# A decoder step on one core: the first x tile's v columns in plain fp32, and a new order of the start

## The chip, the cores and the metric

The kernel runs on one core of a Trainium2 chip. The metric is device time in microseconds (us); of several runs the median counts.

## The reference

`reference()` computes one layer of a hybrid decoder for a prompt of 1024 tokens and for 8 single sample tokens with saved state. All of it is float32, the model width is 1024.

```python
hn = rmsnorm(x, g_norm)                 # x * rsqrt(mean(x*x) + 1e-6) * g_norm
u = hn @ w_in                           # 1024 x 7176: xa za q k v o zb, then 8 gate columns
yA, ... = rglru_branch(xa, ...)         # convolution, two gates, linear recurrence
hB, ... = mlstm_seq(q, k, v, ig, lf, ...)   # 4 heads, chunks of 128 tokens
merged = concat([yA * silu(za), rms(sigmoid(o) * hB) * g_mhead * silu(zb)])
y = rmsnorm(x + merged @ w_out, g_final)
```

The change touches the norm and the first 256 + 256 columns of v (`v0`, `v1`) together with the 8 gate columns.

## The kernel before

**Numbers.** Most products are made of three passes: each float32 operand is split into a rounded high part (a cast on ACT, line 70) and a low part (a subtraction on DVE, line 71), and TensorE adds high·high, high·low and low·high (`mm3`, lines 64 to 66, or `plain`, line 531). A float32 operand that is not split goes through TensorE as it is; the trace then shows two records for each matmul that isn't a transpose.

**The first unit.** The input projection runs in units of two column blocks of 256. Units 1 to 13 use a scheme with seven products on quadrants of x and w (`product`); the seven splits of x quadrants and of their sums stand in `cb`. Unit 0 (`v0 v1`) is computed tile by tile while x is still being normalised: `plain(i, w)` multiplies token tile i (128 tokens) with column block w, and its block w = 0 carries the 8 gate columns as well (264 columns). It is 24 matmuls, k chunks 0 to 3 and then 4 to 7.

**Preparing a tile.** The eight tiles come in the order 4 0 5 1 6 2 7 3 (`xorder`; n counts places in it). `x_fetch(n)` loads a tile. `x_stats(n)` squares it on ACT, takes the root, and finishes the reciprocal root on DVE (n = 0, 1) or on POOL (`rsqrt_early`, n > 1). `x_scale(n)` multiplies by that and by the broadcast g_norm on DVE. `x_turn(n)` transposes it on TensorE in two halves of four. `x_splits(n)` splits the transposed halves from PSUM. `x_copy` copies the halves of a tile i >= 4 for later sums; `x_combos(i)` makes the sums that `product` needs (one subtraction for i >= 4, three for i < 4), and `x_out` splits these. For the first tile the scaling is in `x_turn(0)` (line 425), straight from the PSUM tiles `gn_p` in which a matmul with a row of ones spreads g_norm over all partitions (line 560); `gn_b` is the copy of them for the later tiles.

**What sets the order.** From line 561 to line 638 PE, DVE and ACT run in the order in which the code issues the instructions (`manual_schedule`). In step m of the loop at line 581 `plain(i, 0)` comes first, then the next tile's transposes and splits, then `plain(i, 1)`, and between them statistics, sums and their splits. Before line 561 and after line 638, and on SP and POOL throughout, a list scheduler places the instructions as they become ready. Loads go over SP's DMA queue (`ld`), stores over POOL's (`stq`); only the two halves of g_norm's row go over ACT's queue (line 373). The x tiles and the split weights of block 1 (`w1`) share a ring of six buffers (`ws`).

**The sample tokens.** In steps 2 to 4 the 8 sample tokens are normalised too (`sample_turn`, `sample_square`, `sample_sum`, `sample_scale`, `sample_out`); the last one writes `hnd` on DVE (line 461), which the matmuls of line 604 in step 4 read.

Of the kernel before, what the change touches and what calls it, by code (L numbers as in the profile page):

```python
# [9 lines left out]
F32 = mybir.dt.float32  # L10
# [7 lines left out]
P = 128  # L18
T = 1024
HT = 512  # L20
# [29 lines left out]
def hymba_kernel(  # L50
# [17 lines left out]
    def split(hi, lo, src):  # L68

        A.copy(hi, src)  # L70
        V.tensor_tensor(lo, src, hi.bitcast(F32), op=ALU.subtract)  # L71
# [9 lines left out]
    def ps(tag, shape):  # L81
        return psp.tile(shape, F32, tag=tag, name=f"ps_{tag}", bufs=NBUF.get(tag, 1))
# [13 lines left out]
    def ws(shape, name, dt=F32R):  # L96

        return wsp.tile(shape, dt, tag="ws", name=name)
# [8 lines left out]
    def dconst(shape, name):  # L107

        return dpool.tile(shape, F32, tag=name, name=name)
# [98 lines left out]
    def load_raw(u, b, parts=(0, 1)):  # L208

        if u >= len(units):  # L210
            return
        if (u, b) not in raws:
            raws[u, b] = rawp.tile([P, 4, 512], F32, tag=f"raw{b}", name=f"raw{b}_{u}")
        for a in parts:
            kind, j = units[u][a]
            c = COL[kind] + j * 256
            ld(raws[u, b][:, :, a * 256:(a + 1) * 256],
               w_in[0, b * HT:(b + 1) * HT, c:c + 256].rearrange("(k p) c -> p k c", p=P))
# [151 lines left out]

    gn_r = [sg([1, HT], f"gn_r{n}") for n in range(2)]
    for n in range(2):
        nc.scalar.dma_start(gn_r[n], g_norm[:, n * HT:(n + 1) * HT])
    warm = const([P, 1], "warm")
    A.activation(warm, ones[:, 0:1], AF.Sqrt)
    es_f = ExitStack()
# [4 lines left out]
    xorder = [4, 0, 5, 1, 6, 2, 7, 3]  # L381
    xt, xps, bf = {}, {}, {}

    def x_fetch(n):

        i = xorder[n]
        xt[i] = fp.tile([P, T], F32, tag="x2", name=f"x{i}") if n % 3 == 2 else ws([P, T], f"x{i}", F32)
        ld(xt[i], x_prompt[0, i * P:(i + 1) * P, :])

    def x_scale(n):  # L390
        x = xt[xorder[n]]
        V.scalar_tensor_tensor(x, x, st0[:, 1, n:n + 1], gn_b, op0=ALU.mult, op1=ALU.mult)
# [11 lines left out]
    def x_stats(n):  # L404

        ss, r, t = (st0[:, j, n:n + 1] for j in range(3))
        junk = sg([P, T], "junk", BF16)
        A.activation(junk, xt[xorder[n]], AF.Square, accum_out=ss)
        if n > 1:
            rsqrt_early(r, ss, t)  # L410
            return
        A.activation(r, ss, AF.Sqrt, scale=1.0 / T, bias=eps_t)
        V.tensor_scalar(ss, ss, 1.0 / T, EPS, op0=ALU.mult, op1=ALU.add)
        V.reciprocal(r, r)
        V.tensor_tensor(t, r, r, op=ALU.mult)
        V.scalar_tensor_tensor(t, t, -0.5, ss, op0=ALU.mult, op1=ALU.mult)
        V.scalar_tensor_tensor(r, t, 1.5, r, op0=ALU.add, op1=ALU.mult)
# [45 lines left out]
    def x_split(i, half):  # L463

        p = xps[i][half]
        s = slice(i % 4 * P, (i % 4 + 1) * P)
        if i >= 4 and half == 0:
            bf[i] = [fp.tile([P, 4, P], F32R, tag=f"b12{n}", name=f"b12{n}") for n in "hl"]
            split(*bf[i], p)
        else:  # L470
            q = Q_P3 if i >= 4 else (Q_P1, Q_P2)[half]
            split(cb[q][0][:, :, s], cb[q][1][:, :, s], p)

    def x_copy(i):

        bf["f"] = [sg([P, 4, P], f"b{n}2f") for n in (1, 2)]
        for f, p in zip(bf["f"], xps[i]):
            A.copy(f, p)

    def x_combos(i):  # L480

        p0, p1 = xps[i]
        f0, f1 = bf["f"]
        if i >= 4:
            t3 = sg([P, 4, P], "t3")
            V.tensor_tensor(t3, f1, f0, op=ALU.subtract)
            return [(Q_P7, t3)]
        t1, t2, t4 = (sg([P, 4, P], f"t{n}") for n in (1, 2, 4))
        V.tensor_tensor(t1, f0, p0, op=ALU.subtract)
        V.tensor_tensor(t2, f1, t1, op=ALU.subtract)  # L490
        V.tensor_tensor(t4, p1, t2, op=ALU.subtract)
        return [(Q_P6, t2), (Q_P5, t1), (Q_P4, t4)]

    def x_out(i, ts):

        s = slice(i % 4 * P, (i % 4 + 1) * P)
        for q, t in ts:
            split(cb[q][0][:, :, s], cb[q][1][:, :, s], t)
# [3 lines left out]
    wg = fp.tile([P, KC, 8], F32, tag="wg", name="wg")  # L502
    w1 = []

    def w1_split(b):

        t = ws([P, 4, 256], f"w1h{b}"), ws([P, 4, 256], f"w1l{b}")
        split(t[0], t[1], raws[0, b][:, :, 256:512])
        w1.append(t)

    gs = dconst([P, NCH, 8], "gs")

    def plain(i, w):

        s = slice(i % 4 * P, (i % 4 + 1) * P)
        op = []
        for k in range(KC):
            if i < 4:
                op.append([t[:, k % 4, s] for t in cb[Q_P1 if k < 4 else Q_P2]])
            elif k < 4:  # L520
                op.append([t[:, k, :] for t in bf[i]])
            else:
                op.append([t[:, k % 4, s] for t in cb[Q_P3]])
        pt = ps("o", [P, 512])[:, 0:264 - 8 * w]
        todo = [(k0, x, y) for k0 in (0, 4) for x, y in ((0, 0), (1, 0), (0, 1))]
        if w == 0 and i == xorder[0]:
            todo[1], todo[2] = todo[2], todo[1]
        for k0, x, y in todo:
            for k in range(k0, k0 + 4):
                wt = (hi, lo)[y][:, k, :] if w == 0 else w1[k // 4][y][:, k % 4, :]  # L530
                TE.matmul(pt, op[k][x], wt, start=(k, x, y) == (0, 0, 0), stop=(k, x, y) == (7, 0, 1), skip_group_check=True)  # L531

        def evac():
            t = fp.tile([P, 256], F32, tag="pe", name="pe", bufs=2)
            A.copy(t, pt[:, 0:256])
            if w == 0:
                V.tensor_tensor(gs[:, i, :], pt[:, 256:264], bgate, op=ALU.add)
            stq(d_v[w][i * P:(i + 1) * P, :], t)
        return evac

    pw = ps("tr", [P, P])

    x_fetch(0)
    load_raw(0, 0, (0,))
    ld(wg, w_in[0, :, C_G:C_G + 8].rearrange("(k p) c -> p k c", p=P))
    load_raw(0, 1, (0,))
    load_raw(0, 0, (1,))
    x_fetch(1)
    load_raw(0, 1, (1,))
    ld(xs8, x_sample.rearrange("b o (k p) -> (b o k) p", p=P))  # L550
    ld(g8, g_norm.rearrange("o (k p) -> (o k) p", p=P))
    x_fetch(2)
    ld(bgate[:, 0:4], b_mi[0].partition_broadcast(P))
    ld(bgate[:, 4:8], b_mf[0].partition_broadcast(P))
    x_fetch(3)
    for n in range(10):
        TE.matmul(pw, ones, ones, start=True, stop=True)
        if n == 6:
            for half in range(2):
                TE.matmul(gn_p[half], ones[0:1, :], gn_r[half], start=True, stop=True)  # L560
    ms_ = tc.manual_schedule(engines={mybir.EngineType.PE, mybir.EngineType.DVE, mybir.EngineType.Activation})
# [2 lines left out]
    def w0_split(k):  # L564
        split(hi[:, k:k + 2, 0:256], lo[:, k:k + 2, 0:256], raws[0, k // 4][:, k % 4:k % 4 + 2, 0:256])

    def x_splits(n):
        for half in range(2):
            x_split(xorder[n], half)
    x_stats(0)  # L570
    for half in range(2):
        A.copy(gn_b[:, half * HT:(half + 1) * HT], gn_p[half])
    x_turn(0)
    w0_split(0)
    split(hi[:, :, 256:264], lo[:, :, 256:264], wg)
    w0_split(2)
    x_splits(0)
    w0_split(4)
    w0_split(6)
    ts = []  # L580
    for m, i in enumerate(xorder):
        pe0 = plain(i, 0)
        if m == 0:
            x_stats(1)
            x_scale(1)
            w1_split(0)
            w1_split(1)
        else:
            if m + 2 < 8:
                x_stats(m + 2)  # L590
            if i >= 4:
                x_copy(i)
            else:
                ts = x_combos(i)
        if m + 1 < 8:
            x_turn(m + 1)
        if m == 2:
            sample_turn()
        if m == 3:
            sample_sum()  # L600
        if m == 4:
            pgd = ps("o", [P, 512])[0:32, 0:8]
            for k in range(KC):
                TE.matmul(pgd, hnd[:, k, 8:40], wg[:, k, :], start=k == 0, stop=k == KC - 1)
            dec_unit(0)
            load_raw(1, 0)
            load_raw(1, 1)
        if m + 1 < 8:
            x_splits(m + 1)
        pe0()  # L610
        if m == 2:
            sample_square()
        if m == 3:
            sample_scale()
        if m == 4:
            gd = dconst([NB, 8], "gd")
            V.tensor_tensor(gd, pgd[0:NB], bgate[0:NB], op=ALU.add)
            ld(d_gd, gd)
        if m == 7:
            prep(1, Q_P1)  # L620
        pe1 = plain(i, 1)
        if m == 0:
            x_stats(2)
            x_copy(i)
        if 1 < m + 2 < 8:
            x_scale(m + 2)
        if i >= 4:
            ts = x_combos(i)
        x_out(i, ts)
        pe1()  # L630
        if m == 3:
            sample_out()
        if m < 4:
            x_fetch(m + 4)
# [1026 lines left out]
```

## Time and profile before

| | |
|---|---|
| median of 3 runs | 933.48 us (932.17 to 935.03) |
| profiled execution, device time | 934.05 us |
| its span | 932.3 us |
| PE busy | 919.0 us, 99% of the span |
| PE weight loads (beside PE) | 760.4 us, 82% |
| DVE busy | 706.6 us, 76% |
| ACT busy | 575.4 us, 62% |
| POOL busy | 155.7 us, 17% |
| chain that ended last | PE 92%, DVE 2%, ACT 2%, DMA 2%, issue 1% |

The span goes from the first to the last instruction of the profiled execution; 1.75 us of its device time lie outside. The chain is followed back from the last instruction to what released each one. Times in the rows count from the start of the span.

### The profile page before, as it was taken

To read this page: it belongs to the slowest core of one execution; us is meant where nothing else is said; L and a number is where in the kernel's file an instruction comes from. 1 tells how busy PE (TensorE), PEld (TensorE's weight loads), DVE (VectorE), ACT (ScalarE), POOL (GpSimd) and SP (SyncE) were. 2 spreads that over 40 slices of the span, in tenths; PEclk is the share of its full clock that TensorE was granted. 3 is DMA by queue.
4 is the path that set the end of the run, shared out by engine and by line. 5 is a ranking of instruction groups with operands and counts; after the bars stand their busy time and mean duration, and the time that the engine had idled before them with its cause. 6 is when DMAs were issued, how large, how long until landed. Compare 5 with 4: busy or idle time off the path is not lost.

```text
span 932.3 us, 15295 instructions
## 1 busy us (share of the span) xinstructions
PE 919.0 (99%) x5313; PEld 760.4 (82%) x5313; DVE 706.6 (76%) x1460; ACT 575.4 (62%) x1034; POOL 155.7 (17%) x290
## 2 busy tenths in 40 slices
PE   9999999999999999999999999999999999999996
PEld 7997687878787988687789898876687888888886
DVE  5765887899888888989788866688757677667754
ACT  6743456767686668588577773447636466556642
POOL 1420111011211222222112212010201000000110
PEclk9999999999999999999999999999999999999999
DMA  6341364344566466457726562534963664465431
GB/s 216 107 130 63 128 202 159 119 158 152 186 195 202 164 227 224 154 170 262 229 79 222 175 202 92 170 141 171 346 184 119 161 187 147 126 182 164 122 84 48
DMA packets 131191, 153.17 MB, mean 164 GB/s; under 512 B 15660, under 2 KB 110004, under 8 KB 131106
## 3 DMA queue, kind: packets, MB, share of 16 engines
q1 hardware_dynamic: 113382, 96.32, 34.6%
q0 software_dynamic: 17728, 55.87, 16.5%
q8 instruction: 42, 0.69, 0.3%
q14 instruction: 35, 0.29, 0.1%
q10 hardware_dynamic: 4, 0.00, 0.0%
HBM read 100.58 MB, written 51.65 MB: 163 GB/s over the span
## 4 chain that ended last, share of the span: by engine, by line
PE 92%; DVE 2%; ACT 2%; DMA 2%; issue 1%; SPq 0%; POOL 0%; DVEq 0%; ACTq 0%
PE ps_o L64 14%; PE ps_o L66 14%; PE ps_o L65 14%; PE ps_kv L64 11%; PE ps_kv L66 10%; PE ps_kv L65 10%; PE ps_o L531 4%; PE ps_tr L234 3%; PE ps_s L866 2%; PE ps_s L1196 2%; PE ps_qp L1028 1%; PE ps_tr L1333 1%; PE ps_qp L64 1%; PE ps_qp L65 1%; PE ps_qp L66 1%
## 5 line engine op out<-in xcount | busy, mean ns | idle before, releaser
L70 ACT CAST wh<-raw 128x1024 fp32r<-128x1024 f32 x91 | 95.3, 1048 | 74.8 <-PE ps_o L65 21.0
L71 DVE TENSOR_TENSOR wl<-raw,wh 128x1024 fp32r<-128x1024 f32 x91 | 111.0, 1221 | 35.7 <-ACT wh L70 20.1
L64 PE MATMUL ps_kv<-cb_hi,wh 128*128 128x512 f32 x320 | 126.8, 396 | 0.0
L66 PE MATMUL ps_kv<-cb_hi,wl 128*128 128x512 f32 x320 | 125.3, 391 | 0.0
L65 PE MATMUL ps_kv<-cb_lo,wh 128*128 128x512 f32 x320 | 125.2, 391 | 0.0
L64 PE MATMUL ps_o<-cb_hi,wh 128*128 128x512 f32 x240 | 94.6, 394 | 0.0
L66 PE MATMUL ps_o<-cb_hi,wl 128*128 128x512 f32 x240 | 93.6, 390 | 0.0
L65 PE MATMUL ps_o<-cb_lo,wh 128*128 128x512 f32 x240 | 93.6, 390 | 0.0
L64 PEld LDWEIGHTS ps_kv<-cb_hi,wh 128*128 128x128 f32 x320 | 60.1, 188 | 17.8 <-issue 3.4
L66 PEld LDWEIGHTS ps_kv<-cb_hi,wl 128*128 128x128 f32 x320 | 60.1, 188 | 13.3 <-issue 0.4
L65 PEld LDWEIGHTS ps_kv<-cb_lo,wh 128*128 128x128 f32 x320 | 60.2, 188 | 12.4 <-issue 0.4
L64 PE MATMUL ps_kv<-wh,cb_hi 128*128 128x256 f32 x192 | 54.9, 286 | 0.5 <-ACT s L325 0.5
L66 PE MATMUL ps_kv<-wh,cb_lo 128*128 128x256 f32 x192 | 54.6, 284 | 0.0
L65 PE MATMUL ps_kv<-wl,cb_hi 128*128 128x256 f32 x192 | 54.5, 284 | 0.0
L64 PEld LDWEIGHTS ps_o<-cb_hi,wh 128*128 128x128 f32 x240 | 45.1, 188 | 11.5 <-issue 2.1
L64 PE MATMUL ps_o<-wo,mh 128*128 128x512 f32 (+1 forms) x136 | 53.2, 392 | 1.0 <-ACT mh L70 1.0
L66 PEld LDWEIGHTS ps_o<-cb_hi,wl 128*128 128x128 f32 x240 | 45.1, 188 | 9.7
L64 PE MATMUL ps_o<-wo,rh 128*128 128x512 f32 (+1 forms) x136 | 52.9, 389 | 0.0
L65 PEld LDWEIGHTS ps_o<-cb_lo,wh 128*128 128x128 f32 x240 | 45.1, 188 | 9.1
L66 PE MATMUL ps_o<-wo,rl 128*128 128x512 f32 (+1 forms) x136 | 51.8, 381 | 0.0
L65 PE MATMUL ps_o<-wo,rh 128*128 128x512 f32 (+1 forms) x136 | 51.7, 380 | 0.0
L65 PE MATMUL ps_o<-wo,mh 128*128 128x512 f32 (+1 forms) x136 | 51.5, 380 | 0.0
(492 smaller groups left out, 2447.0 us busy)
## 6 DMA issues: line engine op xcount, KB each, us to landing
raw<-in_w_in_dram SPq DMA_DIRECT2D x56, 512.0 KB
Cb<-in_state_mlstm_C_dram SPq DMA_DIRECT2D x32, 256.0 KB
out_dram<-Cb POOLq DMA_DIRECT2D x32, 256.0 KB, 4.5
qk<-d_qk SPq DMA_DIRECT2D x32, 256.0 KB
oraw<-in_w_out_dram SPq DMA_DIRECT2D x16, 512.0 KB
d_qk<-s POOLq DMA_DIRECT2D x24, 256.0 KB, 3.0
x<-in_x_prompt_dram SPq DMA_DIRECT2D x8, 512.0 KB
d_x<-s POOLq DMA_DIRECT2D x16, 256.0 KB, 3.0
```

The lines of the kernel that those rows point to most:

```text
L64: TE.matmul(out, ah, bh, start=first, stop=False, skip_group_check=True)
L65: TE.matmul(out, ah, bl, start=False, stop=False, skip_group_check=True)
L66: TE.matmul(out, al, bh, start=False, stop=last, skip_group_check=True)
L70: A.copy(hi, src)
L71: V.tensor_tensor(lo, src, hi.bitcast(F32), op=ALU.subtract)
L234: TE.matmul(dz_["p"][32 * g:32 * g + 32, :], hnd[:, k, 0:32] if second else hnd[:, k, 8:40], raws[u, k // 4][:, k % 4, :], start=k < 4 and ...
L531: TE.matmul(pt, op[k][x], wt, start=(k, x, y) == (0, 0, 0), stop=(k, x, y) == (7, 0, 1), skip_group_check=True)
L866: TE.matmul(pg, w[:, n, :], st["xx"][n], start=k == 0, stop=k == 1)
L1028: TE.matmul(pq[32 * g:32 * g + n, 0:256], qsel[:, kb, 4 * bb:4 * bb + n], ds_["C", h * NB + bb][:, kb, :], start=bb < 2, stop=bb >= NB - 2 ...
L1196: TE.matmul(S, qk[:, 2 + kb, :], qk[:, kb, :], start=kb == 0, stop=kb == 1)
L1333: TE.matmul(dec_o[0][32 * g:32 * g + 32, :], md, oraw[m][:, half * 512:(half + 1) * 512], start=first and m in ms[:2], stop=last and m in ...
```

## The change

Nothing changes in the kernel after the start (the loop over units and all that follows). In the start:

- The first tile (tile 4, place 0) goes through both blocks of unit 0 in one function, `first_tile`: its two transposed halves, copied from PSUM as float32, are the stationary operands, and the loaded weights `raws[0, b]` and `wg` the moving ones, none of them split. It is 16 float32 matmuls of 256 columns and 8 of the 8 gate columns, in place of `plain(4, 0)` and `plain(4, 1)`. The weights are still split for the other seven tiles, but `split` of block 1 is taken apart into `w1_hi` and `w1_lo`. Of the first tile only the second half is split (it goes into `cb[Q_P3]`, from the copy).
- g_norm's row is loaded over SP's queue, first in it; the first x tile goes over ACT's queue. The second x tile stands ahead of the weights of block 1. Seven warm-up matmuls in place of ten, and the broadcast of g_norm after five in place of seven.
- The transposes of the second tile come behind `first_tile`.
- In the loop (now steps 1 to 7), `x_combos(i)` and `x_stats(m + 2)` stand later: the statistics behind the next tile's splits, the sums behind `plain(i, 1)`. The first tile's sum is made early and split in step 1.

```diff
     for n in range(2):
-        nc.scalar.dma_start(gn_r[n], g_norm[:, n * HT:(n + 1) * HT])
+        ld(gn_r[n], g_norm[:, n * HT:(n + 1) * HT])
...
-    x_fetch(0)
+    x_fetch(0, nc.scalar.dma_start)
     load_raw(0, 0, (0,))
     ld(wg, w_in[0, :, C_G:C_G + 8].rearrange("(k p) c -> p k c", p=P))
     load_raw(0, 1, (0,))
+    x_fetch(1)
     load_raw(0, 0, (1,))
-    x_fetch(1)
     load_raw(0, 1, (1,))
+    x_fetch(2)
...
-    for n in range(10):
+    for n in range(7):
         TE.matmul(pw, ones, ones, start=True, stop=True)
-        if n == 6:
+        if n == 4:
             for half in range(2):
                 TE.matmul(gn_p[half], ones[0:1, :], gn_r[half], start=True, stop=True)
...
+    def w1_hi(b):
+        t = ws([P, 4, 256], f"w1h{b}"), ws([P, 4, 256], f"w1l{b}")
+        A.copy(t[0], raws[0, b][:, :, 256:512])
+        w1.append(t)
+
+    def w1_lo(b):
+        h, l = w1[b]
+        V.tensor_tensor(l, raws[0, b][:, :, 256:512], h.bitcast(F32), op=ALU.subtract)
...
+    def first_tile():
+        f = bf["f"]
+        pt = [ps("o", [P, 512])[:, 0:264 - 8 * (1 - w)] for w in range(2)]
+        for w in range(2):
+            for k in range(KC):
+                TE.matmul(pt[w][:, 0:256], f[k // 4][:, k % 4, :], raws[0, k // 4][:, k % 4, w * 256:(w + 1) * 256],
+                          start=k == 0, stop=k == KC - 1 and w == 0, skip_group_check=True)
+        for k in range(KC):
+            TE.matmul(pt[1][:, 256:264], f[k // 4][:, k % 4, :], wg[:, k, :], start=False, stop=k == KC - 1, skip_group_check=True)
+        return pt
...
     x_turn(0)
     w0_split(0)
+    x_copy(i0)
+    ts0 = x_combos(i0)
     split(hi[:, :, 256:264], lo[:, :, 256:264], wg)
     w0_split(2)
-    x_splits(0)
+    x_stats(1)
+    x_scale(1)
     w0_split(4)
     w0_split(6)
+    split(cb[Q_P3][0][:, :, 0:P], cb[Q_P3][1][:, :, 0:P], bf["f"][1])
+    pt0 = first_tile()
+    x_turn(1)
+    w1_hi(0)
+    x_stats(2)
+    x_splits(1)
+    w1_hi(1)
+    x_scale(2)
+    w1_lo(0)
+    w1_lo(1)
+    evac0(i0, 0, pt0[0], None)
+    evac0(i0, 1, pt0[1], pt0[1])
+    x_fetch(4)
     for m, i in enumerate(xorder):
+        if m == 0:
+            continue
         pe0 = plain(i, 0)
-        if m == 0:
-            x_stats(1)
-            x_scale(1)
-            w1_split(0)
-            w1_split(1)
-        else:
-            if m + 2 < 8:
-                x_stats(m + 2)
-            if i >= 4:
-                x_copy(i)
-            else:
-                ts = x_combos(i)
+        if i >= 4:
+            x_copy(i)
         if m + 1 < 8:
             x_turn(m + 1)
...
         if m + 1 < 8:
             x_splits(m + 1)
         pe0()
+        if m + 2 < 8:
+            x_stats(m + 2)
...
         pe1 = plain(i, 1)
-        if m == 0:
-            x_stats(2)
-            x_copy(i)
-        if 1 < m + 2 < 8:
+        ts = x_combos(i)
+        if m + 2 < 8:
             x_scale(m + 2)
-        if i >= 4:
-            ts = x_combos(i)
         x_out(i, ts)
+        if m == 1:
+            x_out(i0, ts0)
         pe1()
```

## Rows read from the trace of the kernel before

**Rows 1.** The page: busy time of each engine (share, instructions); granted clock in slices.
```profile
PE 919.0 (99%) x5313; PEld 760.4 (82%) x5313; DVE 706.6 (76%) x1460; ACT 575.4 (62%) x1034; POOL 155.7 (17%) x290
...
PEclk9999999999999999999999999999999999999999
```

**Rows 2.** Timeline, first 24 us, PE: start, us, engine, line, out<-in, shape, count.
```profile
1.14 3.36 PE L557 MATMUL ps_tr<-ones 128*128 128x128 f32 x14 [1.14 <-POOL ones L115]
...
4.43 3.78 PE L560 MATMUL ps_o<-gn_r,ones 1*128 1x512 f32 x4
...
9.58 1.91 PE L429 MATMUL ps_kv<-idF,x 128*128 128x128 f32 x8
...
11.31 1.25 PE L531 MATMUL ps_o<-wph,b12h 128*128 128x264 f32 x4
...
13.24 1.07 PE L531 MATMUL ps_o<-wph,b12l 128*128 128x264 f32 x4
...
14.12 0.67 PE L531 MATMUL ps_o<-wph,cb_hi 128*128 128x264 f32 x4
...
14.63 0.65 PE L531 MATMUL ps_o<-wph,cb_lo 128*128 128x264 f32 x4
...
16.74 0.66 PE L429 MATMUL ps_s<-idF,x 128*128 128x128 f32 x4 [0.98 <-DVE x L392]
...
20.54 0.65 PE L531 MATMUL ps_o<-wph,cb_hi 128*128 128x264 f32 x4
...
23.44 1.04 PE L429 MATMUL ps_kv<-idF,x 128*128 128x128 f32 x8
```

**Rows 3.** Timeline, first 10 us: SP's queue, ACT and DVE.
```profile
0.75 0.40 SPq L388 DMA_DIRECT2D x<-in_x_prompt_dram  x1
...
1.52 1.28 ACT L375 ACT_TABLE_LOAD   x1 [1.52 <-PEq L1647]
...
4.35 1.06 ACT L408 ACTIVATE junk<-x 128x1024 bf16<-128x1024 f32 x1 [1.33 <-DMA x<-in_x_prompt_dram]
...
6.57 0.16 DVE L417 SCALAR_TENSOR_TENSOR st<-st 128x1 f32<-128x1 f32 x1
...
8.24 0.59 ACT L572 COPY gn_b<-ps_o 128x512 f32<-128x512 f32 x1 [1.12 <-PE ps_o L560]
...
8.86 0.75 DVE L425 SCALAR_TENSOR_TENSOR x<-x,st,ps_o 128x512 f32<-128x512 f32 x1 [0.96 <-ACT gn_b L572]
```

**Rows 4.** Timeline at 169 and 568 us, PE: unsplit float32 matmuls and what follows.
```profile
169.47 0.51 PE L918 MATMUL ps_s<-dxs,graw 128*128 128x8 f32 x4
...
169.83 0.49 PE L64 MATMUL ps_o<-cb_hi,wh 128*128 128x512 f32 x1
...
567.86 0.60 PE L1196 MATMUL ps_s<-qk 128*128 128x128 f32 x4
...
568.30 0.38 PE L1198 MATMUL ps_s<-idF,qk 128*128 128x128 f32 x2
```

**Rows 5.** Timeline at 28 us, PE: step 2's `plain`.
```profile
28.64 0.76 PE L531 MATMUL ps_o<-wph,b12l 128*128 128x264 f32 x4 [0.80 <-DVE b12l L71]
```

**Rows 6.** Timeline, 38 to 47 us: step 3 and the start of step 4.
```profile
38.38 1.04 PE L429 MATMUL ps_kv<-idF,x 128*128 128x128 f32 x8
...
39.02 0.59 ACT L70 CAST b12h<-ps_kv 128x512 fp32r<-128x512 f32 x1 [1.13 <-PE ps_kv L429]
...
39.43 0.69 DVE L491 TENSOR_TENSOR t<-ps_qp,t 128x512 f32<-128x512 f32 x1
...
42.10 1.28 DVE L392 SCALAR_TENSOR_TENSOR x<-x,st,gn_b 128x1024 f32<-128x1024 f32 x1
...
43.29 1.89 DVE L71 TENSOR_TENSOR cb_lo<-t,cb_hi 128x512 fp32r<-128x512 f32 x3
...
45.28 0.27 DVE L461 TENSOR_TENSOR hnd<-dqC,dW 128x64 f32<-128x64 f32 x1
...
46.23 0.64 PE L604 MATMUL ps_o<-wg,hnd 128*32 128x8 f32 x15
```

More of the change, by code (lines that the diff above doesn't have):

```diff
@@ L382, in hymba_kernel, with x_fetch @@
     xt, xps, bf = {}, {}, {}
-    def x_fetch(n):
+    def x_fetch(n, ld=ld):
         i = xorder[n]
@@ L503, in hymba_kernel, with evac0 @@
     w1 = []
[L505 to L509, printed above, removed]
     gs = dconst([P, NCH, 8], "gs")
+    def evac0(i, w, pt, pg):
+        t = fp.tile([P, 256], F32, tag="pe", name="pe", bufs=2)
+        A.copy(t, pt[:, 0:256])
+        if pg is not None:
+            V.tensor_tensor(gs[:, i, :], pg[:, 256:264], bgate, op=ALU.add)
+        stq(d_v[w][i * P:(i + 1) * P, :], t)
     def plain(i, w):
@@ L524, in plain @@
         pt = ps("o", [P, 512])[:, 0:264 - 8 * w]
[L525 to L528, printed above, removed]
+        for k0, x, y in [(k0, x, y) for k0 in (0, 4) for x, y in ((0, 0), (1, 0), (0, 1))]:
             for k in range(k0, k0 + 4):
@@ L531, in plain @@
                 TE.matmul(pt, op[k][x], wt, start=(k, x, y) == (0, 0, 0), stop=(k, x, y) == (7, 0, 1), skip_group_check=True)
[L533 to L539, printed above, removed]
+        return lambda: evac0(i, w, pt, pt if w == 0 else None)
     pw = ps("tr", [P, P])
-    x_fetch(0)
+    x_fetch(0, nc.scalar.dma_start)
     load_raw(0, 0, (0,))
@@ L546, in hymba_kernel @@
     load_raw(0, 1, (0,))
+    x_fetch(1)
     load_raw(0, 0, (1,))
-    x_fetch(1)
     load_raw(0, 1, (1,))
+    x_fetch(2)
     ld(xs8, x_sample.rearrange("b o (k p) -> (b o k) p", p=P))
     ld(g8, g_norm.rearrange("o (k p) -> (o k) p", p=P))
-    x_fetch(2)
     ld(bgate[:, 0:4], b_mi[0].partition_broadcast(P))
@@ L569, in x_splits @@
             x_split(xorder[n], half)
+    def first_tile():
[8 more added lines that the diff above has]
+        return pt
+    i0 = xorder[0]
     x_stats(0)
@@ L574, in hymba_kernel @@
     w0_split(0)
+    x_copy(i0)
+    ts0 = x_combos(i0)
     split(hi[:, :, 256:264], lo[:, :, 256:264], wg)
     w0_split(2)
-    x_splits(0)
+    x_stats(1)
+    x_scale(1)
     w0_split(4)
     w0_split(6)
-    ts = []
+    split(cb[Q_P3][0][:, :, 0:P], cb[Q_P3][1][:, :, 0:P], bf["f"][1])
[11 more added lines that the diff above has]
+    x_fetch(4)
     for m, i in enumerate(xorder):
+        if m == 0:
+            continue
         pe0 = plain(i, 0)
-        if m == 0:
-            x_stats(1)
-            x_scale(1)
-            w1_split(0)
-            w1_split(1)
-        else:
-            if m + 2 < 8:
-                x_stats(m + 2)
-            if i >= 4:
-                x_copy(i)
-            else:
-                ts = x_combos(i)
+        if i >= 4:
+            x_copy(i)
         if m + 1 < 8:
```

## The prediction

> **What bounds the kernel now.** I read the page first. TensorE (PE) is busy for 919.0 of 932.3 us, and the granted clock is 9 or more in every slice [rows 1]. So after the start nearly every microsecond is a matmul's, and what the start takes from or adds to PE's time moves the end by as much: DVE at 76% and ACT at 62% matter only where PE waits for them. Next comes the timeline of the first 24 us, PE alone [rows 2]. It shows warm-ups, the spreading of g_norm (4.43), the first tile's transposes (9.58) and its first product at 11.31; a wait of 0.98 us for the second tile's scaling at 16.74; and at 20.54 the second tile's products. The rows also show two levels of speed: four 264-column matmuls take 0.88 us from 13.24 to 14.12, though 24 of the faster kind take 2.90 from 20.54 to 23.44 (0.121 each). That is about a factor of two, the 1.2 and 2.4 GHz levels, though the granted clock of the page does not show it. The higher one comes at about 14.1, 2.8 us after the first product. One more PE wait, 0.80 us at 28.64 [rows 5], ends what PE loses before step 3.
>
> The sum is made against the profiled execution, 934.05 us (span 932.3); the median of the runs is 933.48, 0.57 less, and the difference is carried over to it.
>
> **Step 1, an earlier start.** A 128-column float32 warm-up is two records; 14 records fill 1.14 to 4.43, 0.235 each [rows 2]. Five warm-ups in place of seven bring the g_norm matmuls forward by 4 x 0.235 = 0.94, to 3.49. They take 3.70 as before (4.43 to about 8.13) and end at 7.2; two more warm-ups bring PE to 8.1. The second half of the tile is scaled behind a copy that waits for the g_norm matmul (8.24, then 8.86 to 9.61 [rows 3]); 0.94 less is 7.9 to 8.7. The first half needs the reciprocal root, ready at 6.73 (line 417, 6.57 + 0.16), so PE can transpose at 8.1, and the eight transposes, 0.24 each at the lower level, end at 10.1. First product at about 10.2 in place of 11.31: -1.1. That the float32 copies take the place of casts costs nothing: 9.58 plus the four transposes to the first product is the same path. Bounds: 0 if g_norm's row comes late over SP's queue, -1.3 if the copies are quicker than casts.
>
> x now shares the DMA engines with the weights: it is issued at 0.75 and lands at 4.35, and so far the weights stood behind it in SP's queue. If x were to land at 5.2, its first half would be scaled at about 8.4 in place of 8.1, and the second transposes would still end near 10.3. So up to there it is covered by PE's own work at the lower level; past it each microsecond costs one.
>
> The page "DMA: Bandwidth & Descriptors" of the Trainium skill (section "Queues, rings and completion order") says that each DMA engine takes turns, packet by packet, between the queues that have work. By it x on ACT's queue must share with the weights on SP's, which the trace of before cannot show, since there both stood in one queue. With 512 KB each, and x some 0.85 us ahead, it would land near 5.2 as an estimate, which is still the covered case, so the sum stays; but it speaks against this part of the change and for rival C below.
>
> **Step 2, the first tile in float32.** Removed: 48 matmuls at 0.121, 5.8 us at the higher level. Added: 16 float32 matmuls of 256 columns. The trace has none, but it has 128-column ones: four records in 0.44 (567.86 to 568.30 [rows 4]), 0.11 a record, 0.22 a matmul, so 0.44 for 256 columns and 7.0 for 16. The 8 gate columns were nearly free inside 264; now they are 16 records of their own with a full 128x128 weight load each. Four of that form take 0.36 (169.47 to 169.83 [rows 4]), 0.09 each: 1.4 us. Together 8.5, +2.7 us. Bounds for the gates: 0.1 us in all if only the columns counted, 2.0 by the row's own 0.51 for four; I take 1.4, which is the same form measured start to start.
>
> The lower level costs, before, 2.8 us x (1 - 0.121/0.22) = 1.25. After, at half speed from 10.2 to the rise: 1.4 if the rise again comes 2.8 us after the first product (13.0, which I take: what the engine does before it is the same, only earlier), 1.95 if it stays at 14.1, 0 if it comes at once.
>
> So `first_tile` ends at 10.2 + 8.5 + 1.4 = 20.1, and the second tile's transposes (0.88 for eight) at 21.0. Before, they lay ahead of block 1 of the first tile, and 2.9 us of matmuls covered the splits behind them; now nothing does. A cast starts 0.64 after the first transpose (38.38 to 39.02 [rows 6]) and needs 0.6, so the next product starts 1.3 after the transposes start, 0.4 after PE is free, and the low part 0.2 later than PE wants it. Its products therefore stand where they would with a start at 21.6, against 20.54: +1.1 (+1.6 with the rise at 14.1). The 0.98 wait of 16.74 is gone in this number already.
>
> **Step 3, the splits ahead of the sums in step 1.** The wait at 28.64 is for a low part that stood behind three sums on DVE. With the sums behind `plain(0, 1)` it goes: -0.8 by the row, -0.9 with the gap that it leaves in the pitch; 0 if block 1's subtractions (2 x 1.2 us, now also there) push it back.
>
> **Step 4, the same move in steps 2 to 7.** The sums (three of 0.7 us for tiles 0 to 3) used to fill DVE while PE was in `plain(i, 0)`, ahead of the next transposes; now they come behind the statistics, and the scaling of the tile after next comes behind both. Step 3 from its transposes X = 38.38 [rows 6]: before, sums done at X + 1.7, scaling from X + 3.7 to X + 5.0, `hnd` ready at X + 7.2. After: casts X + 0.64 to X + 1.7, evacuation, the square (1.06) and the root to X + 3.4; DVE has finished the two low parts at X + 2.9 and waits for the root; then the sample tokens' small work, 0.8; sums X + 4.2 to X + 6.3; scaling to X + 7.5. PE wants that tile at X + 0.9 + 0.2 + 48 x 0.121 = X + 6.9: a wait of 0.6 to 0.7. Then three low parts (1.9) and `hnd` (0.27) to X + 9.7, while PE stands before line 604 at X + 7.5 + 1.0 = X + 8.5: a wait of 1.1. Behind that matmul on PE are the decode matmuls and `plain(6, 1)`, so the end waits too. Steps 1 and 5 have no sample work: about 0.1 each. Together +2.0. Bounds: 0, if PE arrives later than I have it, to +3.0, if POOL's five small operations, which stand between root and scaling, run late in all three odd steps.
>
> Of the rest, split weights, the deferred split of the first tile's sum (0.6 on DVE, step 1) and the second x tile's earlier load lie beside PE's work in stretches where DVE has slack (until 20 it only waits for PE): 0 each, and at most the 0.6 if it hits step 2's splits.
>
> **Sum:** +1.1 - 0.9 + 2.0 = +2.2 us: 936.25 by the profiled execution, 935.7 by the median. With the rise at 14.1 it is +2.7.
>
> **Rivals.**
> A. The new order costs nothing (+1.1 - 0.9 = +0.2: 933.7; 934.2 with the late rise). For it: DVE is at 76%, and before, PE shows no wait for it after 28.64. Against: the step 3 chain has no slack in my sum, because DVE sits waiting for the root at its head.
> B. The higher level is there when the first tile begins, and the order costs nothing: 0.2 - 1.4 = -1.2, 932.3. For: it came 2.8 us after steady products once, and PE is busy from 1.14 on. Against: it was as busy from 1.14 in the kernel before.
> C. x lands late, the other side. ACT's queue is in order: if x's load is issued behind the table load and warm-up activation (to about 3.0 [rows 3]) in place of 0.75, it lands 2.3 later plus up to 1.6 for sharing all of its 512 KB, at 6.6 to 8.3. From 5.2 on this counts: +1.4 to +3.1, so with the sum +3.6 to +5.3, about 938. For: it stands behind that activation in the code. Against: the activation waits for a constant, the load for nothing, and the scheduler places what is ready.
> D. The lower level lasts through the whole float32 tile: the work after 13.0, 7.1 us at full speed, takes twice as long: +7.1, with the sum +9.3, 942.8. For: 3.3 us of float32 warm-ups left the level low. Against: later float32 work runs at the higher one.
>
> **Chances.** The forecast 0.56, A 0.20, B 0.10, C 0.09, D 0.05. A measurement of this kernel tells about 0.3%, 2.8 us, from no change. The forecast with its rise between 13.0 and 14.1 and the bounds of step 4 lies mostly inside it, but about a third (0.19) above; C and D are slower; A lies inside, B inside but for 0.04; 0.01 more for what I don't see. Faster 0.05, same 0.62, slower 0.33. The range leaves out part of B, D and the far end of C: 932.4 to 938.0.
>
> **What would show it.** Step 1: the first float32 product at 10.2. Step 2: records of 0.22 after the rise and 0.45 before, gates at 0.09, the end of the tile near 20.1. Step 3: no wait at the place of 28.64. Step 4: PE waits of 0.6 for the scaling before step 4's transposes (`x_turn(5)`) and of 1.1 for line 461 before line 604's matmuls. PE's busy time 1.5 to 3 us up shows the exchange itself. The prediction is wrong if the second tile's products start before 20.5, or if step 4's waits are absent.

## The result, and the profile of the changed kernel

The change makes the kernel slower: 938.07 us (median of 8 runs, 935.32 to 938.62) against 933.8 for the kernel before beside it, a ratio of 1.0045, 95% interval [1.0032, 1.0057], or +4.2 us [+3.0, +5.3]. Run again in a later batch it gave 937.41, ratio 1.0043 [1.0028, 1.0058]. Forecast were +2.2 and 935.7, with 938.0 as the upper end of the range. The profiled execution took 938.02 (span 936.3, before 932.3): 4.0 us of span to account for.

The page's first lines and its granted clock:
```profile
PE 922.5 (99%) x5307; PEld 760.8 (81%) x5307; DVE 705.1 (75%) x1459; ACT 574.7 (61%) x1033; POOL 154.6 (17%) x290
...
PEclk9999999999999999999999999999999999999999
```
PE is busy 3.5 us longer than in [rows 1] with six records fewer. That looks like longer matmuls. The clock line says nothing: a slice is 23 us long, and what matters below takes a seventh of one. Below, the rise is the moment at the start from which records take half as long, and a fall is a later stretch in which the granted clock reads 0.50.

The timeline of PE in the first 32 us (start, us, engine, line, out<-in, shape, count):
```profile
8.30 1.91 PE L429 MATMUL ps_kv<-idF,x 128*128 128x128 f32 x8
10.03 2.49 PE L579 MATMUL ps_o<-raw,b12f 128*128 128x256 f32 x8
12.36 1.89 PE L579 MATMUL ps_o<-raw,b22f 128*128 128x256 f32 x8
...
17.54 0.95 PE L582 MATMUL ps_o<-wg,b12f 128*128 128x8 f32 x8
...
19.24 0.64 PE L429 MATMUL ps_s<-idF,x 128*128 128x128 f32 x4
...
20.55 0.76 PE L530 MATMUL ps_o<-wph,cb_hi 128*128 128x264 f32 x4 [0.24 <-ACT cb_hi L70]
...
23.81 1.04 PE L429 MATMUL ps_kv<-idF,x 128*128 128x128 f32 x8
...
28.04 0.64 PE L530 MATMUL ps_o<-wph,b12l 128*128 128x264 f32 x4
...
31.26 0.63 PE L429 MATMUL ps_s<-idF,x 128*128 128x128 f32 x4 [0.65 <-DVE x L392]
```
The first product starts at 10.03 (11.31 before). The float32 tile with its gates ends at 19.24, and the second tile's products start at 20.55, where they stood before [rows 2], ending 0.37 later (23.81 against 23.44). The wait of [rows 5] is gone (28.04), and a new one has come at 31.26.

x's load and the first use of x, timeline of ACT (ACTq is its queue):
```profile
0.74 0.38 ACTq L388 DMA_DIRECT2D x<-in_x_prompt_dram  x1
...
4.41 1.06 ACT L408 ACTIVATE junk<-x 128x1024 bf16<-128x1024 f32 x1 [1.77 <-DMA x<-in_x_prompt_dram]
```
x is issued when it was before, and its first use is at 4.41 instead of 4.35 [rows 3].

Steps 3 and 4, timelines of PE and of DVE:
```profile
38.67 1.06 PE L429 MATMUL ps_kv<-idF,x 128*128 128x128 f32 x8
...
46.42 0.63 PE L429 MATMUL ps_s<-idF,x 128*128 128x128 f32 x4 [0.68 <-DVE x L392]
...
48.41 0.80 PE L626 MATMUL ps_o<-wg,hnd 128*32 128x8 f32 x15 [0.92 <-ACT cb_hi L70]
...
49.12 3.32 PE L234 MATMUL ps_tr<-raw,hnd 128*32 128x512 f32 x13
52.37 0.74 PE L530 MATMUL ps_o<-w1h,b12h 128*128 128x256 f32 x4
```
```profile
45.00 1.27 DVE L392 SCALAR_TENSOR_TENSOR x<-x,st,gn_b 128x1024 f32<-128x1024 f32 x1
46.19 1.89 DVE L71 TENSOR_TENSOR cb_lo<-t,cb_hi 128x512 fp32r<-128x512 f32 x3
48.01 0.26 DVE L461 TENSOR_TENSOR hnd<-dqC,dW 128x64 f32<-128x64 f32 x1
```
The two waits forecast are there: 0.68 for the scaling and 0.92 before the matmul with `hnd`. The second is put down to a cast, but `hnd` itself ends at 48.27 and PE starts 0.14 later: it is the last to come. After them 13 decode matmuls (line 234, for the sample tokens) take 3.32 us. In the kernel before they took 1.88, and PE had no wait in step 4:
```profile
45.26 0.60 PE L429 MATMUL ps_s<-idF,x 128*128 128x128 f32 x4
...
46.76 1.88 PE L234 MATMUL ps_tr<-raw,hnd 128*32 128x512 f32 x13
48.57 0.74 PE L531 MATMUL ps_o<-w1h,b12h 128*128 128x256 f32 x4
```
Short windows of the changed kernel say why. A row has the window, its length, the busy time and instructions of PE, PEld, DVE, ACT and POOL, then the granted clock, the DMA share and GB/s:
```profile
48.00:49.00 1.00, 0.59 (x14) 0.62 (x15) 1.00 (x4) 1.00 (x3) 0.16 (x1) 0.81 0.11 37
49.00:50.00 1.00, 1.00 (x13) 0.40 (x16) 0.58 (x3) 0.89 (x3) 0.40 (x1) 0.50 0.07 25
50.00:51.00 1.00, 1.00 (x12) 0.39 (x8) 0.77 (x3) 0.20 (x1) 0.83 (x3) 0.50 0.31 107
51.00:52.00 1.00, 1.00 (x9) 0.00 (x0) 0.32 (x1) 0.42 (x1) 0.47 (x3) 0.50 0.00 0
52.00:53.00 1.00, 1.00 (x9) 0.63 (x6) 1.00 (x2) 0.00 (x0) 0.00 (x0) 0.99 0.67 146
```
At about 48.6, 0.2 us after the second wait has ended, the clock falls from 2.4 to 1.2 GHz (0.50 of full speed), and it comes back at about 52. Nothing in the prediction had this.

The +4.0 against the rows of before: +0.4 for start and first tile together (23.81); -1.0 for the wait of 28.64; +0.7 and +0.2 for the new wait at 31.26 and smaller ones up to step 3 (38.67 against 38.38 [rows 6]); +0.9 at the scaling wait of step 4 (46.42 against 45.26) and +1.0 at `hnd`, which makes +2.2 there (48.41 against 46.23 [rows 6]); +1.6 for the matmuls at the lower level (52.37 against 48.57); +0.2 later.

### The profile page after: what moved, and what is told of

Read it like the earlier page. It is cut to its first block, busy times and chain, and to the rows that moved or that the text cites. A ratio compares the mean times of both kernels' runs of the same rounds, so it can differ in the third digit from the quotient of the medians.

```text
span 936.3 us, 15278 instructions
## 1 busy us (share of the span) xinstructions
PE 922.5 (99%) x5307; PEld 760.8 (81%) x5307; DVE 705.1 (75%) x1459; ACT 574.7 (61%) x1033; POOL 154.6 (17%) x290
## 4 chain that ended last, share of the span: by engine, by line
PE 93%; ACT 3%; DVE 2%; issue 1%; DMA 1%; POOL 0%; DVEq 0%; ACTq 0%; SPq 0%; POOLq 0%
PE ps_o L64 14%; PE ps_o L66 14%; PE ps_o L65 14%; PE ps_kv L64 11%; PE ps_kv L66 10%; PE ps_kv L65 10%; PE ps_tr L234 3%; PE ps_o L530 3%; PE ps_s L888 2%; PE ps_s L1218 2%; PE ps_qp L1050 1%; PE ps_tr L1355 1%; PE ps_qp L64 1%; PE ps_qp L65 1%; PE ps_qp L66 1%
```

## The experiments

Ratios are to the kernel before in the same batch (933.5, 934.0 and 933.5 us). The two further profiles of the kernel before are single executions, without a ratio.

**The changed kernel with the old order of the loop; the float32 tile stays.**
```diff
         pe0 = plain(i, 0)
+        if m + 2 < 8:
+            x_stats(m + 2)
         if i >= 4:
             x_copy(i)
+        else:
+            ts = x_combos(i)
...
         pe0()
-        if m + 2 < 8:
-            x_stats(m + 2)
...
-        ts = x_combos(i)
         if m + 2 < 8:
             x_scale(m + 2)
+        if i >= 4:
+            ts = x_combos(i)
```


> The changed kernel with the loop's old order (statistics and sums ahead of the next transposes), the float32 first tile kept. Theory 1 (the new order makes PE wait three times, 0.65, 0.68 and 0.92 us, and the level falls to 0.50 for 3.3 us behind them, 1.6 us more): no wait before steps 2 and 4's transposes nor before the matmuls that read hnd, granted clock 1.00 from 45 to 62 us, a wait near 28 us back (0.8), and 934 to 935 against 933.8 before. Rival (the 2.8 us that float32 adds to PE's work is the loss): stays at 937 to 938.

934.18 us, ratio 1.0005 [0.9994, 1.0016]: the loss is gone with the order, and start and float32 tile together cost nothing that can be told from none. Its first product and the places of the two waits of step 1, on PE's timeline:
```profile
10.03 3.45 PE L579 MATMUL ps_o<-raw,b12f 128*128 128x256 f32 x8
13.32 1.89 PE L579 MATMUL ps_o<-raw,b22f 128*128 128x256 f32 x8
...
21.51 0.76 PE L530 MATMUL ps_o<-wph,cb_hi 128*128 128x264 f32 x4 [0.24 <-ACT cb_hi L70]
...
24.78 1.04 PE L429 MATMUL ps_kv<-idF,x 128*128 128x128 f32 x8
...
29.07 0.76 PE L530 MATMUL ps_o<-wph,b12l 128*128 128x264 f32 x4
...
31.61 0.60 PE L429 MATMUL ps_s<-idF,x 128*128 128x128 f32 x4
```
Eight records take 3.45 us where the changed kernel's took 2.49: here the higher level came at about 13.2, there at about 11.2, with the same code in front. The second tile's products then start at 21.51, about where step 2 of the prediction had them (21.6). Two things came out otherwise than expected: the wait of [rows 5] does not come back with the old order (the low part's matmuls start at 29.07 without a recorded wait), and PE still waits 0.45 before the matmuls with `hnd` (47.18). The profile has no fall.

**The kernel before with the new order alone.**
```diff
-        else:
-            if m + 2 < 8:
-                x_stats(m + 2)
-            if i >= 4:
-                x_copy(i)
-            else:
-                ts = x_combos(i)
+        elif i >= 4:
+            x_copy(i)
...
         pe0()
+        if m > 0 and m + 2 < 8:
+            x_stats(m + 2)
...
+        if m > 0:
+            ts = x_combos(i)
         if 1 < m + 2 < 8:
             x_scale(m + 2)
```


> The kernel before with only the loop's new order. Theory 1: the wait at 28.6 us goes (-0.9), the waits for the scaling and for hnd come (about +2.3), and with them the low level of 3.3 us (+1.6): 936.5 to 937.5 against 933.8, granted clock 0.50 near 49 us. Rival (the float32 tile is the loss): 933 to 934.

935.86 us, ratio 1.0022 [1.0012, 1.0033]. The waits of PE between 15 and 50 us are now these four:
```profile
16.73 0.66 PE L429 MATMUL ps_s<-idF,x 128*128 128x128 f32 x4 [1.29 <-DVE x L392]
30.56 0.63 PE L429 MATMUL ps_s<-idF,x 128*128 128x128 f32 x4 [0.31 <-DVE x L392]
45.51 0.63 PE L429 MATMUL ps_s<-idF,x 128*128 128x128 f32 x4 [0.68 <-DVE x L392]
47.60 0.61 PE L599 MATMUL ps_o<-wg,hnd 128*32 128x8 f32 x15 [1.03 <-ACT cb_hi L70]
```
The first is no cost: its transposes start where they did before (16.73 against 16.74 [rows 2]), and PE only came to them sooner. The wait of [rows 5] is gone, and the other three put the matmuls with `hnd` at 47.60 instead of 46.23 [rows 6], 1.4 later; the span is 1.5 longer. So the order costs about what its waits cost. This profile has no fall, so the part of theory 1 that hung on it is not seen, and the time lies under its 936.5 to 937.5. +2.1 for the order and +0.5 for the rest make 2.6 and not 4.2, though the two intervals leave room for it.

**The changed kernel, `sample_out` moved ahead of `x_out`.**
```diff
+        if m == 3:
+            sample_out()
         x_out(i, ts)
...
-        if m == 3:
-            sample_out()
```


> The changed kernel with hnd's write ahead of the three low parts of step 3 on DVE. Theory 1: the wait of 0.92 us before the matmuls that read hnd goes, the 0.68 before the transposes stays; if the level fell because PE stood idle in both, it now stays at 1.00 and the decode matmuls take 1.9 us in place of 3.4: 935.5. If the level falls with whatever runs there (narrow decode matmuls), only 0.9 goes: 937.1, granted clock still 0.50 near 49 us.

935.23 us, ratio 1.0020 [1.0008, 1.0033]. The wait for `hnd` is gone (line 626 starts at 48.40 although the higher level came late in this profile, at about 13.3, which puts the rest 1 us later), the waits of 0.65 and 0.68 stay, and the clock reads 1.00 up to 931 us. That is theory 1's time (935.5). But this profile has the late rise, and no other profile with a rise between 12.4 and 14.1 has a fall in step 4 either, so it does not show that the missing wait kept the clock up.

**The changed kernel with PE kept busy in both waits of step 4.** First with 3 and 4 float32 matmuls of ones:
```diff
+        if m == 4:
+            pw2 = ps("tr", [P, P])
+            for n in range(3):
+                TE.matmul(pw2, ones, ones, start=True, stop=True)
         if m + 1 < 8:
             x_turn(m + 1)
...
         if m == 4:
+            for n in range(4):
+                TE.matmul(pw2, ones, ones, start=True, stop=True)
```


> The changed kernel with seven more 128-column float32 matmuls of ones, three before step 4's transposes and four before the matmuls that read hnd, 0.22 us each, into a PSUM tile that nobody reads: they lie in waits of 0.68 and 0.92 us. Theory 1 (idle PE lets the level fall): granted clock 1.00 throughout, decode matmuls 1.9 us, 936.4, that is 1.6 below the changed kernel though PE does 1.5 us more. Rival (the level falls with the narrow matmuls, or for another reason): 0.50 near 49 us again, 938.

937.62 us, ratio 1.0044 [1.0028, 1.0061]. Its profiled execution (936.09) shows 1.00 from 45 to 62, but it is one with a late rise (about 12.9), and the median is that of the changed kernel: this fill doesn't hold the clock for most runs, or their clock falls elsewhere, or it costs what it saves.

Then with 5 and 7 matmuls of the split form, 256 columns, in the same two places.
```diff
+            for n in range(5):
+                TE.matmul(pw2[:, 0:256], cb[Q_P1][0][:, n % 4, 0:P], w1[0][0][:, n % 4, :], start=True, stop=True)
...
+            for n in range(7):
+                TE.matmul(pw2[:, 0:256], cb[Q_P1][0][:, n % 4, 0:P], w1[0][0][:, n % 4, :], start=True, stop=True)
```


> The changed kernel with 5 and 7 split-form matmuls of 256 columns (0.12 us each), whose results are not read, in the PE waits before x_turn(5) and before the decode gate product; nothing is left out. If the kind of work in this stretch (float32 transposes and narrow float32 matmuls) lets the clock fall, dense wide matmuls hold it: no stretch of the lower level between 45 and 62, waits shortened to 0.3 or less, runs within 935.4 to 936.8. Rival (the fall depends on the run and not on this stretch, or idle time is not the cause): the runs spread over 935 to 939 again and the median is 937.5 or more.

938.79 us, ratio 1.0058 [1.0038, 1.0077], runs of 937.3 to 939.5: the rival's numbers. The profiled execution (937.34) has a rise at about 13.3 and no fall, and is no faster for it. The kind of matmul in this stretch isn't what decides the median.

**The changed kernel with the statistics back in their old place and `sample_out` early; the splits stay ahead of the sums.** To the edit of the experiment with `sample_out` this adds:
```diff
         pe0 = plain(i, 0)
+        if m + 2 < 8:
+            x_stats(m + 2)
...
         pe0()
-        if m + 2 < 8:
-            x_stats(m + 2)
```


> The changed kernel with two pieces put back: the statistics of the tile after next stand ahead of the next tile's copy and transposes again, and the decode sample (hnd) ahead of the sums in step 3; the splits stay ahead of the sums, the float32 first tile stays. Theory 1 (what the change loses after the start is the order's: waits of 0.65, 0.68 and 0.92 us and the lower level behind them): each of the three waits falls to 0.4 or less, no stretch of the lower granted clock between 45 and 62, and the time is 933 to 934.3 (the start and the float32 tile are worth between -0.6 and +0.3 with the wait at 28.64 gone). Theory 2 (the float32 tile itself, 2.8 us of more PE time, is the loss): the waits may go, but the time stays at 936 or more.

934.67 us, ratio 1.0015 [1.0003, 1.0027], in one batch with the changed kernel at 937.41: the two pieces put back give 2.7 us, a little less than theory 1 wanted (933 to 934.3), and theory 2 (936 or more) is out. None of the waits of 0.65, 0.68 and 0.92 is left; in step 4:
```profile
45.62 0.60 PE L429 MATMUL ps_s<-idF,x 128*128 128x128 f32 x4
...
46.59 0.64 PE L628 MATMUL ps_o<-wg,hnd 128*32 128x8 f32 x15
```
Its clock does fall once, earlier (below).

**The changed kernel again, for a second profile.**

> The changed kernel itself, beside the others on one chip. If the fall of the granted clock at 48 to 52 belongs to the kernel, its profile shows it again and the median is 937 to 938.5. If it depends on the run, the profile may lack it, and its span is then about 1.6 us below 936.3 (934.7, or 935.9 with a later rise in the first tile), while the median stays where it was.

937.41 us. The profile (937.11, span 935.3) has the two waits of step 4 but no fall there; the 13 decode matmuls take 1.88 us. The fall is at 20.5 instead, at the second tile's products:
```profile
10.03 2.07 PE L579 MATMUL ps_o<-raw,b12f 128*128 128x256 f32 x8
...
21.91 1.08 PE L530 MATMUL ps_o<-wpl,cb_hi 128*128 128x264 f32 x4
22.79 1.08 PE L530 MATMUL ps_o<-wph,cb_hi 128*128 128x264 f32 x4
...
48.83 0.61 PE L626 MATMUL ps_o<-wg,hnd 128*32 128x8 f32 x15 [0.92 <-ACT cb_hi L70]
...
49.33 1.88 PE L234 MATMUL ps_tr<-raw,hnd 128*32 128x512 f32 x13
```
The windows have 0.50, this one and the next:
```profile
21.00:22.00 1.00, 1.00 (x6) 1.00 (x6) 1.00 (x2) 1.00 (x3) 0.00 (x0) 0.50 0.66 172
```
From 20.5 to 23.9 PE is at the lower level, and groups of four split matmuls take 1.08 for 0.65. So the place of the fall belongs to the execution, not to step 4. With PE held up here, the wait of 0.65 in step 1 is gone: the transposes start at 31.67 without a recorded wait. This profile (rise at 10.4) makes a clean pair with the one of the experiment before (934.56): rise and fall are at nearly the same places in both (10.6 and 20.6 there), and the difference is 2.55 us.

**Two further profiles of the kernel before**, nothing changed.

> The kernel before itself, for a second profile of it (the first one has its higher level from 14.1 on and no granted clock under 0.99 in its first 100 us). If the stretch of the lower level belongs to the changed kernel alone, no profile of before shows one there. If it comes in any kernel, in the runs in which the higher level comes early, a profile with a rise before 12.5 has such a stretch too, of about the 3.3 us that the changed kernel's had.

> The same kernel a third time, with the same expectations: the rise falls early or late from one execution to the next, so one profile may show only one of the two.

The first took 932.12 (span 930.3), the second 934.50 (932.7). PE's timeline and the windows of the first:
```profile
4.42 1.98 PE L560 MATMUL ps_o<-gn_r,ones 1*128 1x512 f32 x4
6.33 0.94 PE L557 MATMUL ps_tr<-ones 128*128 128x128 f32 x6
7.75 1.64 PE L429 MATMUL ps_kv<-idF,x 128*128 128x128 f32 x7 [0.48 <-issue]
```
```profile
8.00:10.00 2.00, 2.00 (x10) 1.76 (x9) 2.00 (x5) 1.16 (x3) 0.00 (x0) 0.50 1.08 388
10.00:12.00 2.00, 2.00 (x14) 2.00 (x13) 1.99 (x4) 2.00 (x4) 0.00 (x0) 0.68 1.10 353
```
Here the higher level is there at 4.4: the g_norm matmuls take 1.98 us for 3.78 [rows 2], and the first product starts at 9.42, 1.9 earlier. The clock then falls at 7.8, after the gap of 0.48, and is back at 11.3. It falls where the execution of [rows 2] was at the lower level anyway (to 14.1), so against that one nothing is lost, and the span is 2.0 us shorter. The second has no such stretch, a rise at about 12.6, and the waits at the old places (16.73 and 28.63).

**The kernel before with only the parts that take time away.** g_norm first on SP's queue, x over ACT's, five warm-ups, splits ahead of the sums, `sample_out` early; no float32 tile, statistics where they were.
```diff
-        nc.scalar.dma_start(gn_r[n], g_norm[:, n * HT:(n + 1) * HT])
+        ld(gn_r[n], g_norm[:, n * HT:(n + 1) * HT])
...
-    x_fetch(0)
+    x_fetch(0, nc.scalar.dma_start)
...
-    for n in range(10):
+    for n in range(7):
...
-            else:
-                ts = x_combos(i)
...
+        if i < 4:
+            ts = x_combos(i)
...
+        if m == 3:
+            sample_out()
         x_out(i, ts)
```


> The kernel before with only the parts of the change that took time away: g_norm's row first on SP's queue, x's first tile over ACT's queue, the second x tile's load earlier, five warm-ups in place of seven ahead of the spreading, and the splits ahead of the sums, with the statistics where they were and hnd ahead of the sums; no float32 first tile. Theory 1: -0.9 to -1.2 for the earlier start, -1.0 for the wait at 28.64, nothing given back: 931 to 932. Rival (the early start is lost again because the splits of the first tile, the weights or the lower level of the clock then set the pace, as in a later rise): 933 to 934, the same as before.

933.30 us, ratio 0.9999 [0.9985, 1.0012]. The time is the rival's. The profile has most of theory 1's gain (932.57, span 930.8, 1.5 under the first profile of before, both without a fall inside PE's work), with the wait of 28.64 exchanged for another one:
```profile
29.73 0.63 PE L429 MATMUL ps_s<-idF,x 128*128 128x128 f32 x4 [0.76 <-DVE x L392]
```
The median shows no gain: the kernel before has executions like the first further profile above, and this one has some at 934.6 to 935.9.

**The same, with step 1's scaling ahead of the sums.**
```diff
+        if m == 1:
+            x_scale(3)
         if i < 4:
             ts = x_combos(i)
-        if 1 < m + 2 < 8:
+        if 1 < m + 2 < 8 and m != 1:
             x_scale(m + 2)
```


> The kernel of the experiment with only the saving parts (no float32 tile), and in step 1 the scaling of the tile after next ahead of the three sums. Theory: its wait of 0.76 at 29.73 is the three sums (26.26 to 28.3) standing ahead of that scaling, whose statistic was there at 24.5, so it goes, with nothing late instead: span 930.0 to 930.2, time 931.8 to 932.6, some 1 us under the kernel before. Rival: the sums' splits, now 1.2 us later, make the second half of step 1 wait, and the time stays at 933.3.

934.46 us, ratio 1.0009 [0.9995, 1.0022]: the gain isn't there. The wait for the scaling at 29.73 is gone; the second half of those transposes now waits 0.31 for the sums (29.74), and one of 1.22 comes at 45.22, again for a scaling. The profiled execution (937.07) has its fall at about 289.5, behind another wait:
```profile
289.00 0.50 PE L868 MATMUL ps_s<-xl,ghi 128*128 128x512 f32 x1 [2.44 <-ACT ig L822]
```
By the medians no version tried is faster than the kernel before.

## Why the prediction missed

Two things failed: step 4's price for step 1 of the loop (0.1, where the wait is 0.65), and the sum's silence on the clock after its first rise, which it put at nothing. Against the 936.25 forecast for the profiled execution, 938.02 is 1.8 more: -0.7 in start and first tile, -0.1 in step 3, +0.8 in step 4, +1.6 for the fall, +0.2 later.

**Steps 1 to 3 were about right.** Step 1: first product at 10.03 (10.2 forecast), x used at 4.41, so rival C is out. Step 2: records of 0.216 at the higher level and 0.43 at the lower (0.22 and 0.45), gates 0.106 each, 1.7 us in all for 1.4. With the rise at 13.2 the second tile's products start at 21.51 (21.6) and end at 24.78; in the profiled execution the rise came at 11.2, and they start at 20.55 and end at 23.81. Against 23.44 the term is +1.3 or +0.4 for +1.1, by the execution. That the profiled one got +0.4 is luck. Rival B is out, since in none of the nine profiles with the changed start does the rise come before the first tile begins, and so is D. Step 3: -1.0 for -0.9, but that the order earned it isn't shown: with the old order and the float32 tile (the first experiment) the wait is gone too, since PE comes to it 1.3 later.

The Trainium skill's rule on turns between queues ("DMA: Bandwidth & Descriptors", section "Queues, rings and completion order") would have put x near 5.2 as an estimate. Of the nine profiles with the changed start eight have x's first use at 4.31 to 4.50 and one, the first experiment's, at 4.93, with its first product at 10.03 all the same; with the old start it is at 4.32 to 4.44. A delay to 5.2 isn't seen.

**Step 4 was undersized: +2.8 where +2.0 was forecast** (inside its bounds of 0 to +3.0). That the order costs something is shown by the order alone, +2.1 [+1.1, +3.1], so rival A is out. The two waits in the kernel's step 4 were sized right (0.68 for 0.6 to 0.7; 0.92 for 1.1). "Steps 1 and 5 [...] about 0.1 each" failed for step 1: its wait is 0.65. The chain, ACT and then DVE:
```profile
25.95 0.37 ACT L510 COPY pe<-ps_o 128x256 f32<-128x256 f32 x1 [0.42 <-DMA d_v<-pe]
26.21 1.06 ACT L408 ACTIVATE junk<-x 128x1024 bf16<-128x1024 f32 x1
```
```profile
27.73 0.17 DVE L397 RECIPROCAL st<-st 128x1 f32<-128x1 f32 x1 [1.10 <-ACT st L396]
27.81 0.67 DVE L489 TENSOR_TENSOR t<-b12f,ps_s 128x512 f32<-128x512 f32 x1
...
29.84 1.27 DVE L392 SCALAR_TENSOR_TENSOR x<-x,st,gn_b 128x1024 f32<-128x1024 f32 x1
```
The evacuation waits 0.42 for a transfer out of its buffer, the square stands behind it on ACT, the root behind the square, and on DVE the sums and the scaling behind the root: DVE idles 1.10, and PE pays 0.65. The first experiment and the one with `sample_out` have nearly the same rise (13.2 and 13.3) and no fall: with the old order there is no wait here, with the new one 0.65. In the kernel without the float32 tile, with early statistics but the sums still ahead of the scaling, it is 0.76 (29.73, the saving parts alone), and with the scaling first it is gone. So there the sums ahead of the scaling are enough to make PE wait. The late statistics are a second reason: in the clean pair this scaling starts at 30.25 with them and at 29.46 with early ones. For the waits of step 4 the clean pair shows it: both are gone with the statistics and `sample_out` put back.

**The missing term is the clock after its first rise: +1.6 in the profiled execution.** The prediction weighed the level only up to its first rise and took 1.00 from there on. Thirteen profiles say otherwise. In the four with a rise at 11.2 or earlier (the changed kernel twice, the version with early statistics, the first further profile of before) a fall follows, at 48.6, 20.5, 20.6 and 7.8, each behind a wait of PE of 0.24 to 0.92 us. Waits of the same length stand without a fall in the other profiles (0.24 at 21.51 in the first experiment, for one). In eight of the nine with the rise at 12.4 or later there is none before PE's work ends; the ninth, the last version, falls at 289.5 behind a wait of 2.44, so an early rise isn't needed for it. What a fall costs depends on where it lies: in before it lies on the start, and that execution is still the fastest of the three; in step 4 it costs 1.6 us; at 20.5 the second tile's products take 4.6 us for 3.3, but the wait of 0.65 behind them is then gone.

In these profiles a fall before 50 us comes only with the early rise, and the two partly cancel. The experiment with `sample_out` has neither (rise at 13.3): 936.47, or about 937.5 with the 1.0 of `hnd` put back, an estimate of the changed kernel as the prediction imagined its clock. So of the 1.8 us missed in the profiled execution some 1.2 stand without any fall, mostly in step 4, and rise and fall together add about 0.5.

The mean granted clocks of the runs fit this. Of 72 runs of the kernel before, 36 have 0.998 or more (median 933.99); of the 36 at 0.997 or less, 24 lie at 930.8 to 932.9, like the first further profile, and 12 at 933.7 to 938.6. Of 15 runs of the changed kernel, 6 have 0.998 or more (median 936.83) and 9 less, at 937.1 to 939.6. Compared at 0.998 or more the change costs 936.83 - 933.99 = 2.8 us, near the +2.2 forecast; the rest of the +4.2 would be that no run of it profits from an early level as a third of those before do, and more than half pay for a fall. This sorts runs after the fact, over several batches; it is no experiment.

**Open:** why a rise at 4.4 wasn't seen with the change. One of three profiles of before has it and none of the nine with the changed start, which has five warm-ups before g_norm's matmuls where before had seven; whether that moves it wasn't tested. Neither was what places the fall: two fills of the waits in step 4 didn't bring the median down, so idle time there isn't shown to be the cause.

## What to carry to other kernels

Where an engine's queue is in order, a chain that is moved (square, root, scaling) must be priced with everything now in front of it on each queue, an evacuation that waits for a transfer included, and not by its own length. When PE is the bound, look at the granted clock in windows of 1 us around each new wait and each stretch that got earlier; the page's slices are too wide for it. And one profile is one execution: where runs of one kernel differ by 5 us, take two or three profiles before blaming a line for the last 2 us.

## What the runs showed of the hardware

The moment of the first rise of TensorE's clock isn't fixed by the program: the same code went to the higher level at 4.4, 12.6 or 14.1 (before), and at 10.4 or 11.2 (the changed kernel). The lower level at the start isn't shown by the granted clock (1.00 between 8 and 14 us of the first profile of before, where records take twice their time); a later fall is shown as 0.50. Float32 products of 256 columns take 0.216 us a record, two records each, at the higher level; with 8 columns 0.106 a record with its own weight load.
